# Second attention: three PSUM banks for the turned probabilities and factors, two for the projections

## The chip, the cores and the metric

The kernel runs on one core of one Trainium2 chip. The metric is the device time of one execution in microseconds (us). TensorE (PE in the profile) multiplies matrices and writes its results to PSUM, which has eight banks, each 128 partitions by 512 float32 values. VectorE (DVE) and ScalarE (ACT) read the banks; GpSimd (POOL) works in SBUF alone here; SyncE (SP) issues the loads of weights.

## The reference

Two blocks run one after the other on 512 tokens of width 1024. The first (gated linear attention, stick-breaking attention, an MLP) is not touched. The second, cut to what matters:

```python
def nsa_mixer(h, w_in, w_out, k_pos, k_w1, k_w2, v_pos, v_w1, v_w2, table):
    q, kv, g, z = split_cols(h @ w_in, [NSA_WIDTH, 6 * NSA_KV_WIDTH, 3 * H, 3 * NSA_WIDTH])
    k_c, v_c, k_s, v_s, k_w, v_w = [...]
    gates = jax.nn.sigmoid(g).reshape(B, S, 3, H, 1)
    zs = jax.nn.silu(z).reshape(B, S, 3, H, dh)
    kc = compress_kv(k_c, k_pos, k_w1, k_w2)
    vc = compress_kv(v_c, v_pos, v_w1, v_w2)
    o_cmp, p_cmp = nsa_compressed(q, kc, vc, table)
    o_slc = nsa_selected(q, k_s, v_s, select_blocks(p_cmp, S), table)
    o_win = nsa_window(q, k_w, v_w, table)
    o = jnp.stack([o_cmp, o_slc, o_win], axis=2)
    y = jnp.sum(gates * o * zs, axis=2).reshape(B, S, NSA_WIDTH)
    return y @ w_out
```

There are 16 heads in 4 groups. `z` holds one gate projection for each of the three branches: 24 products of 128 columns by 512 tokens, for 8 pairs of heads `p` and 3 branches `br`.

## The kernel before

The second attention is the function `nsa`. Everything on TensorE there stands in one order, written out by the program: the pieces of attention itself, and between them a **filler** (the class `Filler`), which deals out the steps of the remaining projections so that TensorE always has something to do. TensorE works through its instructions strictly in that order. The orders of VectorE and ScalarE are made by a scheduler when the program is built.

One **unit** of attention (class `Unit`) is a head and a branch. `scores` multiplies queries and keys into a bank of the ring `sc` (lines 1217, 1218); VectorE takes the minimum (L1220) and ScalarE the exponential into `P` (L1223). Two steps later `flip` turns `P` by multiplications with the identity into a bank of the ring `tp` (L1237); ScalarE copies it out as the high part of `ptall` (L1240) and VectorE subtracts that for the low part (L299, names `ptall<-b,ptall`). Later `mix` multiplies it with the values into bank 6 (L1253).

The **filler's** steps are projections of eight k-tiles with three multiplications each (L339, L340, L341, by `gen_t`). `project(p, br)` makes one gate projection: its bank comes from `pj`, and when it is full, ScalarE takes the tanh of it (L995) and VectorE multiplies (L296, names `z<-z,b`). Only then is the bank free. Keys and queries are projected in the same way (their readings are L853 and L875 on ScalarE, L296 `q<-b,q` on VectorE), and `cmp_hidden` (L942 to L944) makes the hidden layer of the compression in a bank of `pj`, woven into a projection by `both`.

Small pieces are hung into a projection by `weave`: after the third of its eight steps (`SH` and `FH` are 2) comes `cmp_scores` (L1050) or `cmp_flip` (L1080). Their bank comes from `mx`, which is the same ring as `pj`. `combine(p)` says which projection of a pair has one. `gate_flip` (L1135), `gate_scale` (L1145) and `finish` (L1092) multiply gate factors and take their banks from `tp`.

A ring deals out its banks in turn, whoever asks:

```python
            bank, sc, tp, av = ring(0, 1, 7), ring(2, 3), ring(4, 5), ring(6)
...
            mx = bank
...
                elif p == 2:
                    order = ((1, {FH: lambda: flip(0)}), (2, score(1, 0)), (0, score(1, 1)))
```

The first multiplication into a bank waits until the last reader of what the bank held has ended, and everything behind it on TensorE waits as well.

Of the kernel before, what the change touches and what calls it, by code (L numbers as in the profile page):

```python
# [245 lines left out]
def emit(gen):  # L246
    for _ in gen:
        pass
# [3 lines left out]
def tile_blocks(ctx, tc, x, xt, wts, prm, cst, table, post_g, w2k, w2v, out):  # L252
# [5 lines left out]
    W = Weights(nc, glob, wts)  # L258
    banks = ctx.enter_context(tc.tile_pool(name="banks", bufs=1, space=PSUM))

    def ring(*ids):
        turn = [0]

        def take():
            i = ids[turn[0] % len(ids)]
            turn[0] += 1
            return banks.tile([128, T], F32, name=f"b{i}", tag=f"b{i}", bufs=1)
        return take
# [20 lines left out]
    def ts(out_, in_, s1, s2=None, op0=OP.mult, op1=None, eng=None):  # L289
        if s2 is None:  # L290
            (eng or v).tensor_scalar(out_, in_, s1, None, op0)
        else:
            (eng or v).tensor_scalar(out_, in_, s1, s2, op0, op1)  # L293

    def stt(out_, a, sc, b, op0, op1):
        v.scalar_tensor_tensor(out_, a, sc, b, op0, op1)  # L296

    def tt(out_, a, b, op=OP.mult, eng=None):
        (eng or v).tensor_tensor(out_, a, b, op)  # L299

    def hi_lo(hi, lo, src, hi_in=None, scale=None):
        if scale is None:
            s.copy(hi, src)
            tt(lo, src, hi.bitcast(F32), OP.subtract)
        else:
            s.activation(hi, src, AF.Identity, scale=scale)
            stt(lo, src, scale, hi.bitcast(F32), OP.mult, OP.subtract)
# [18 lines left out]
    def act_tiles(kt):  # L326
        h = glob.tile([128, T], F32R, name=f"ah{kt}", tag="ah", bufs=8)
        l = glob.tile([128, T], F32R, name=f"al{kt}", tag="al", bufs=8)
        return h, l
# [22 lines left out]
    def gen_n(psum, acts, evac, tail=1, w=512):  # L352
        n = len(acts) // 2
        ps = [psum() for _ in range(4)]
        held = []
        for k2 in range(n):
            wh, wl = W.next()
            if k2 < n - tail:
                order = [(k2, wh, wl, k, tb) for k in range(2) for tb in range(4)]
            else:  # L360
                held.append((k2, wh, wl))
                if k2 < n - 1:
                    continue
                order = [(*w, k, tb) for tb in range(4) for w in held for k in range(2)]
            for kk, wh, wl, k, tb in order:
                ah, al = acts[2 * kk + k]
                tsl = slice(128 * tb, 128 * tb + 128)
                a = wh[:, w * k:w * k + w]
                b = wl[:, w * k:w * k + w]
                o = ps[tb][:, 0:w]  # L370
                end = kk == n - 1 and k == 1
                pe.matmul(o, ah[:, tsl], a, start=(kk == 0 and k == 0), stop=False)  # L372
                pe.matmul(o, ah[:, tsl], b, start=False, stop=False)  # L373
                W.last = pe.matmul(o, al[:, tsl], a, start=False, stop=end)  # L374
                if end:
                    evac(tb, ps[tb])
                yield 650.0
# [403 lines left out]
    def nsa(x2, ssq2):  # L781
# [3 lines left out]
        kst, qst = {}, {}  # L785
        with ExitStack() as pts:
            pt = pts.enter_context(tc.tile_pool(name="pt", bufs=1))
            bank, sc, tp, av = ring(0, 1, 7), ring(2, 3), ring(4, 5), ring(6)

            opened, when, used = [0], [0], [0]  # L790

            def pj():
                opened[0] += 1
                when[0] = fill.ticks
                return bank()

            mx = bank

            acts = [act_tiles(kt) for kt in range(KT)]
# [50 lines left out]
            def keys_evac(gq):  # L850
                def evac(ps):
                    ks = tmp("ks")
                    s.copy(ks, ps)  # L853
                    for br in range(2):
                        kh = pn.tile([128, T], F32R, name="kh", tag="kh", bufs=4)
                        kl = pn.tile([128, T], F32R, name="kl", tag="kl", bufs=4)
                        src = ks[64 * br:64 * br + 64, :]
                        same = slice(64 * br, 64 * br + 64)
                        for d_ in range(2):
                            s.copy(kh[64 * d_:64 * d_ + 64, :], src)  # L860
                        for d_ in range(2):
                            tt(kl[64 * d_:64 * d_ + 64, :], src, kh[same, :].bitcast(F32), OP.subtract)
                        kst[gq, br] = (kh, kl)
                return evac
# [4 lines left out]
            def queries_evac(m):  # L869
                def evac(ps):  # L870
                    for e in range(2):
                        q = pn.tile([128, T], F32R, name="q", tag="qy", bufs=QB)
                        a = slice(64 * e, 64 * e + 64)
                        b = slice(64 - 64 * e, 128 - 64 * e)
                        s.activation(q[a, :], ps[a, :], AF.Copy, scale=-0.125)  # L875
                        stt(q[b, :], ps[a, :], -0.125, q[a, :].bitcast(F32), OP.mult, OP.subtract)
                        qst[2 * m + e] = q
                return evac
# [4 lines left out]
            def values(br):  # L883
                def evac(tb, ps):
                    src = ps[:, 0:256].rearrange("p (g d) -> p g d", g=4)
                    hi = vst[:, tb, 4 * br:4 * br + 4, 0:64]
                    gs = gn[:, tb, 24 * br:24 * br + 24]
                    s.activation(gs, ps[:, 256:280], AF.Tanh, scale=0.5)
                    ts(gs, gs, 0.25, 0.25, OP.mult, OP.add)
                    s.copy(hi, src)  # L890
                    tt(vst[:, tb, 4 * br:4 * br + 4, 64:128], src, hi.bitcast(F32), OP.subtract)
                emit(gen_n((ring(3, 4, 5, 6), ring(2, 0, 1, 7))[br], acts, evac, w=280))
                if br == 0:
                    ts(gn[:, 0, 0:16], gn[:, 0, 0:16], valid)

# [55 lines left out]
                yield 1300.0  # L951

            def cmp_middle(th):
                pst = mx()
                for k in range(2):
                    pe.transpose(pst[:, 128 * k:128 * k + 128], th[:, 128 * k:128 * k + 128], ident)
                hT = pt.tile([128, 256], F32, name="hT", tag="z", bufs=ZB)
                ts(hT, pst[:, 0:256], 0.5)
                return hT
# [1 line left out]
            pct = {}  # L961

            def cmp_output(i, hT, w2):
                o = mx()
                for k in range(2):
                    if i == 0:
                        pe.matmul(o[:, 0:128], w2[:, k, :], hT[:, 128 * k:128 * k + 128],
                                  start=(k == 0), stop=(k == 1))
                    else:
                        pe.matmul(o[:, 0:64], hT[:, 128 * k:128 * k + 128], w2[:, k, :],  # L970
                                  start=(k == 0), stop=(k == 1))
                if i == 0:
                    hi_lo(kc[:, :, 0, :], kc[:, :, 1, :], o[:, 0:128].rearrange("p (g c) -> p g c", g=4))
                else:
                    vc = glob.tile([128, 128], F32, name="vc", tag="dg", bufs=2)[:, 0:64]
                    v.tensor_copy(vc, o[:, 0:64])
                    tc.keep_in_program_order(g.memset(vcb, 0.0))
                    pct["v"] = vc
# [30 lines left out]
            def early():  # L1009
                st = {}  # L1010

                def middle():
                    st["hT"] = cmp_middle(st["th"])

                def output(i):
                    cmp_output(i, st["hT"], st[i])
                Fs, st[0] = yield from compress(0)
                yield from both(cmp_hidden(Fs, st), project(0, 0))
                Fs, st[1] = yield from compress(1, ({2: middle}, {2: lambda: output(0)}))
                started[0] = True  # L1020
                yield from both(cmp_hidden(Fs, st), queries(4))
                yield from weave(keys(2), {2: middle, 5: lambda: output(1)})
                spread_values(0)
                spread_values(1)
# [237 lines left out]
            def attention(fill):  # L1262
# [70 lines left out]
                while pend_flip or pend_mix:  # L1333
# [4 lines left out]
                    pend_mix += new  # L1338

            first = [(pj(), W.next(1), keys_evac(0)), (pj(), W.next(1), queries_evac(0)),  # L1340
                     (mx(), W.next(1), queries_evac(1))]
            enter(0)
            for kt in range(KT):
                if kt == ENTER:
# [11 lines left out]
            for br in range(2):  # L1356
                values(br)
# [38 lines left out]
    with tc.manual_schedule(engines={mybir.EngineType.PE, mybir.EngineType.Pool}):  # L1396
        nsa(xb, sums2)
# [55 lines left out]
```

## Time and profile before

| what | us |
|---|---|
| median of 3 runs | 1370.8 (1369.51 to 1370.91) |
| the profiled execution | 1372.04 |
| its span, first to last instruction | 1370.3 |
| TensorE busy in the span | 1324.2 (97%) |
| VectorE, ScalarE, GpSimd busy | 728.0, 656.0, 273.7 |
| second attention with its filler, 938 to 1320 us: TensorE busy | 359.34 of 382.00 |

A row of the timeline says when an instruction started (us from the start of the span), how long it took, its engine, line, operation, and what it writes from what; in square brackets stands how long its engine had been idle, and what ended that. Names of PSUM buffers are cut to `b`.

### The profile page before, as it was taken

The numbers are of one execution on the slowest core, as the hardware profiler recorded it, in microseconds if no ns is written. First come the engines' busy times: TensorE is split into PE (matmuls) and PEld (weight loads), VectorE is DVE, ScalarE is ACT, GpSimd is POOL, SyncE is SP. The second block draws the span as 40 slices with busy tenths as digits, with TensorE's granted clock in tenths as the row PEclk, the third lists the DMA queues.
The fourth block names the chain that finished last, engine by engine and source line by source line (L and its number), as shares of the span: only waits on it lengthen the run. The fifth ranks groups of instructions, "written<-read, shape, count | busy, mean of one in ns | idle before, by whom it ended". The sixth has DMA issues, their size and how long they took to land.

```text
span 1370.3 us, 17904 instructions
## 1 busy us (share of the span) xinstructions
PE 1324.2 (97%) x6670; PEld 1090.5 (80%) x6670; DVE 728.0 (53%) x1386; ACT 656.0 (48%) x1281; POOL 273.7 (20%) x243
## 2 busy tenths in 40 slices
PE   9999999999999999999999999999888999999998
PEld 7977887777786888888888888888667788888776
DVE  4689435656567535342233322545785766665623
ACT  6588624544434326351135512355556556665532
POOL 0023101110101000000000000145536344335342
PEclk9999999999999999999999999999999999999999
DMA  7411221213131424863333324323313122211132
GB/s 236 139 46 49 76 93 55 85 62 93 51 103 47 155 61 133 125 183 94 96 102 93 95 94 129 118 64 119 94 55 111 52 63 62 70 62 63 47 108 77
DMA packets 40695, 125.31 MB, mean 91 GB/s; under 512 B 4528, under 2 KB 9184, under 8 KB 40352
## 3 DMA queue, kind: packets, MB, share of 16 engines
q1 hardware_dynamic: 39696, 119.98, 27.7%
q0 software_dynamic: 912, 4.19, 2.3%
q8 instruction: 52, 0.85, 0.3%
q14 instruction: 35, 0.29, 0.1%
HBM read 115.77 MB, written 8.39 MB: 91 GB/s over the span
## 4 chain that ended last, share of the span: by engine, by line
PE 66%; issue 15%; DVE 10%; ACT 5%; POOL 2%; DMA 1%; SPq 0%; POOLq 0%; DVEq 0%; ACTq 0%
PE b L374 9%; PE b L372 9%; PE b L373 9%; PE b L339 9%; PE b L340 9%; PE b L341 9%; PE b L1253 2%; PE b L1237 2%; DVE b L1220 1%; DVE ptall L299 1%; ACT P L1223 1%; PE b L1217 1%; PE b L828 1%; PE b L1218 1%; DMA xk<-in_xt_dram 1%
## 5 line engine op out<-in xcount | busy, mean ns | idle before, releaser
L171 ACT CAST wh<-wr 128x1024 fp32r<-128x1024 f32 (+3 forms) x204 | 207.8, 1019 | 403.1 <-PE b L374 225.6
L339 PE MATMUL b<-ah,wh 128*128 128x512 f32 x808 | 331.9, 411 | 2.8 <-ACT ks L853 2.4
L173 DVE TENSOR_TENSOR wl<-wr,wh 128x1024 fp32r<-128x1024 f32 (+2 forms) x142 | 169.5, 1195 | 296.9 <-ACT wh L171 296.4
L341 PE MATMUL b<-ah,wl 128*128 128x512 f32 x808 | 317.4, 393 | 0.0
L340 PE MATMUL b<-al,wh 128*128 128x512 f32 x808 | 317.0, 392 | 0.0
L173 POOL TENSOR_TENSOR wl<-wr,wh 128x1024 fp32r<-128x1024 f32 (+1 forms) x62 | 141.8, 2292 | 192.3 <-ACT wh L171 168.3
L341 PEld LDWEIGHTS b<-ah,wl 128*128 128x128 f32 x808 | 152.2, 188 | 32.4
L339 PEld LDWEIGHTS b<-ah,wh 128*128 128x128 f32 x808 | 152.6, 189 | 30.6 <-ACT ks L853 2.6
L340 PEld LDWEIGHTS b<-al,wh 128*128 128x128 f32 x808 | 152.8, 189 | 25.4 <-issue 1.9
L372 PE MATMUL b<-wh,ah 128*128 128x512 f32 (+3 forms) x352 | 125.5, 358 | 1.6 <-ACT wh L171 1.1
L373 PE MATMUL b<-wl,ah 128*128 128x512 f32 (+3 forms) x352 | 125.4, 356 | 0.1
L374 PE MATMUL b<-wh,al 128*128 128x512 f32 (+3 forms) x352 | 125.3, 356 | 0.1
L1223 ACT ACTIVATE P<-b,nm 128x128 f32<-128x128 f32 (+3 forms) x128 | 67.7, 529 | 80.3 <-DVE nm L1220 77.0
L374 PE MATMUL b<-wh,hl 128*128 128x512 f32 x256 | 101.2, 396 | 0.0
L373 PE MATMUL b<-wl,hh 128*128 128x512 f32 x256 | 101.2, 395 | 0.0
L372 PE MATMUL b<-wh,hh 128*128 128x512 f32 x256 | 101.2, 395 | 0.0
L299 DVE TENSOR_TENSOR ptall<-b,ptall 128x128 fp32r<-128x128 f32 (+3 forms) x128 | 62.5, 489 | 62.3 <-ACT ptall L1240 61.4
L1220 DVE CUSTOM_DVE_ANT_0 b<-b,bt 128x128 f32<-128x128 f32 (+3 forms) x128 | 63.1, 494 | 24.4 <-PE b L1218 24.2
L372 PEld LDWEIGHTS b<-wh,ah 128*128 128x128 f32 x352 | 66.2, 188 | 9.9 <-ACT wh L171 1.3
L374 PEld LDWEIGHTS b<-wh,al 128*128 128x128 f32 x352 | 66.4, 189 | 8.4 <-DVE al L296 0.5
L373 PEld LDWEIGHTS b<-wl,ah 128*128 128x128 f32 x352 | 66.4, 189 | 8.4 <-DVE wl L173 0.5
L299 POOL TENSOR_TENSOR rsr<-rsm,mhalf 128x2 f32<-128x2 f32 (+1 forms) x3 | 2.4, 806 | 336.1 <-DVE rsm L293 336.1
(301 smaller groups left out, 2163.7 us busy)
## 6 DMA issues: line engine op xcount, KB each, us to landing
wr<-in_wts_dram SPq DMA_DIRECT2D x188, 512.0 KB, 3.6
bt_d<-tr POOLq DMA_DIRECT2D x4, 768.0 KB, 21.9
wr<-in_wts_dram SPq DMA_DIRECT2D x8, 280.0 KB, 2.6
xk<-in_xt_dram SPq DMA_DIRECT2D x8, 256.0 KB, 3.8
xn<-in_x_dram SPq DMA_DIRECT2D x4, 512.0 KB, 4.7
xbig<-in_x_dram SPq DMA_DIRECT2D x1, 2048.0 KB, 9.4
x_d<-xbig SPq DMA_DIRECT2D x8, 256.0 KB, 3.1
bt<-bt_d SPq DMA_DIRECT2D x8, 256.0 KB, 3.2
```

The lines of the kernel that those rows point to most:

```text
L171: nc.scalar.copy(hi, raw)
L173: eng.tensor_tensor(lo, raw, hi.bitcast(F32), OP.subtract)
L299: (eng or v).tensor_tensor(out_, a, b, op)
L339: pe.matmul(o, a, ah, start=(kt == 0), stop=False)
L340: pe.matmul(o, a, al, start=False, stop=False)
L341: pe.matmul(o, b, ah, start=False, stop=(kt == KT - 1))
L372: pe.matmul(o, ah[:, tsl], a, start=(kk == 0 and k == 0), stop=False)
L373: pe.matmul(o, ah[:, tsl], b, start=False, stop=False)
L374: W.last = pe.matmul(o, al[:, tsl], a, start=False, stop=end)
L1220: v.tensor_tensor_reduce(S[:, 0:n], S[:, 0:n], self.bt[:, h % 2, 512 - n:512], 1.0, -NEG, OP.add, OP.min, nm)
L1223: latest[0] = s.activation(P[:, 0:n], S[:, 0:n], AF.Exp, bias=nm, scale=-1.0, accum_out=self.dn[:, tb, br, h % 2:h % 2 + 1])
L1237: pe.transpose(pst[:, 128 * sb:128 * sb + 128], P[:, 128 * sb:128 * sb + 128], ident)
```

## The change

The rings of the second attention are dealt differently: bank 7 goes from `bank` (projections, compressed scores, turned compressed probabilities) to `tp` (turned probabilities, turned gate factors, products of the factors). Two small users of `mx`, `cmp_middle` and `cmp_output`, now ask `tp`. The third of the three projections that start the block takes bank 6 instead of bank 7, and so the two sets of rings for `values` exchange 6 and 7.

```diff
-            bank, sc, tp, av = ring(0, 1, 7), ring(2, 3), ring(4, 5), ring(6)
+            bank, sc, tp, av = ring(0, 1), ring(2, 3), ring(4, 5, 7), ring(6)
...
-                emit(gen_n((ring(3, 4, 5, 6), ring(2, 0, 1, 7))[br], acts, evac, w=280))
+                emit(gen_n((ring(3, 4, 5, 7), ring(2, 0, 1, 6))[br], acts, evac, w=280))
...
             def cmp_middle(th):
-                pst = mx()
+                pst = tp()
...
             def cmp_output(i, hT, w2):
-                o = mx()
+                o = tp()
...
             first = [(pj(), W.next(1), keys_evac(0)), (pj(), W.next(1), queries_evac(0)),
-                     (mx(), W.next(1), queries_evac(1))]
+                     (av(), W.next(1), queries_evac(1))]
```

No instruction is added or removed, and TensorE's order stays as it was. What moves is the bank that each writes, and with it what each waits for. In the rows below `b7_8900` is bank 7, buffer 8900, and the brackets name the engine whose count is waited for.

TensorE, where the first gate projection of pair 1 (`b0_8785`) ends and the second begins, before:

```order
L339 MATMUL b0_8785<-ah6_6867,wh_8570 128x512
L340 MATMUL b0_8785<-al6_6868,wh_8570 128x512
L341 MATMUL b0_8785<-ah6_6867,wl_8571 128x512
L1237 MATMUL b4_8871<-ident_65,P_8737 128x128 [waits DVE_49]
L339 MATMUL b0_8785<-ah7_6869,wh_8570 128x512
L340 MATMUL b0_8785<-al7_6870,wh_8570 128x512
L341 MATMUL b0_8785<-ah7_6869,wl_8571 128x512
L1217 MATMUL b2_8886<-kh_7274,q_7192 128x128 [waits Activation_49]
L1218 MATMUL b2_8886<-kl_7275,q_7192 128x128
L339 MATMUL b7_8900<-ah0_6855,wh_8623 128x512
```

And the same place of the changed kernel:

```order
L339 MATMUL b0_8785<-ah6_6867,wh_8570 128x512
L340 MATMUL b0_8785<-al6_6868,wh_8570 128x512
L341 MATMUL b0_8785<-ah6_6867,wl_8571 128x512
L1237 MATMUL b4_8871<-ident_65,P_8737 128x128
L339 MATMUL b0_8785<-ah7_6869,wh_8570 128x512
L340 MATMUL b0_8785<-al7_6870,wh_8570 128x512
L341 MATMUL b0_8785<-ah7_6869,wl_8571 128x512
L1217 MATMUL b2_8886<-kh_7274,q_7192 128x128 [waits Activation_49]
L1218 MATMUL b2_8886<-kl_7275,q_7192 128x128
L339 MATMUL b0_8900<-ah0_6855,wh_8623 128x512 [waits DVE_49]
```

The turning of probabilities (L1237) lost its wait for VectorE; the second projection now begins in bank 0, which the first has just filled, and waits for VectorE.

TensorE where `cmp_hidden` of the keys opens its bank, before:

```order
L339 MATMUL b0_7866<-ah1_6857,wh_7579 128x512
L340 MATMUL b0_7866<-al1_6858,wh_7579 128x512
L341 MATMUL b0_7866<-ah1_6857,wl_7580 128x512
L1237 MATMUL b5_7873<-ident_65,P_7744 128x128 [waits DVE_49]
L1237 MATMUL b5_7873<-ident_65,P_7744 128x128 x3
L942 MATMUL b1_7880<-wh_7633,Fh_7730 128x256
```

The same rows of the changed kernel:

```order
L339 MATMUL b0_7866<-ah1_6857,wh_7579 128x512
L340 MATMUL b0_7866<-al1_6858,wh_7579 128x512
L341 MATMUL b0_7866<-ah1_6857,wl_7580 128x512
L1237 MATMUL b7_7873<-ident_65,P_7744 128x128 [waits DVE_49]
L1237 MATMUL b7_7873<-ident_65,P_7744 128x128 x3
L942 MATMUL b1_7880<-wh_7633,Fh_7730 128x256 [waits DVE_49]
```

The hidden layer stays in bank 1, but with two banks in the ring that bank is the one of the projection just before it, and the first multiplication waits for VectorE.

VectorE's order moves by a place or two at eight places; the one at the end of the second projection of pair 1 (`z<-z,b_8900`) as a piece of the difference:

```order
 L299 TENSOR_TENSOR Pc<-Pc,rgc 128x512
-L1220 ISA b_9007,nm<-b_9007,bt 128x128
-L1220 ISA nm 128x1
 L296 SCALAR_TENSOR_TENSOR z<-z,b_8900 128x512
 L299 TENSOR_TENSOR ptall<-b_8992,ptall 128x128
+L1220 ISA b_9007,nm<-b_9007,bt 128x128
+L1220 ISA nm 128x1
```

The reading that frees a projection's bank moved ahead of the minimum over one tile of scores.

## Rows read from the trace of the kernel before

**Rows 1.** The page, busy time by engine.

```profile
PE 1324.2 (97%) x6670; PEld 1090.5 (80%) x6670; DVE 728.0 (53%) x1386; ACT 656.0 (48%) x1281; POOL 273.7 (20%) x243
```

**Rows 2.** Busy times of the second attention: PE, PEld, DVE, ACT, POOL, clock, DMA, GB/s.

```profile
938.00:1320.00 382.00, 359.34 (x2045) 301.34 (x2044) 257.51 (x638) 226.20 (x554) 161.85 (x98) 0.99 0.22 68
```

**Rows 3.** Waits of TensorE from 938 to 1320 us: total, times, longest.

```profile
PE b L1237 <- DVE ptall L299: 7.6, 12, 1.6
PE b L1135 <- DVE ptall L299: 5.3, 2, 3.5
PE b L339 <- ACT ks L853: 2.4, 1, 2.4
PE b L1253 <- DVE t L299: 2.3, 2, 1.5
...
PE b L1092 <- DVE z L299: 0.9, 1, 0.9
PE b L1145 <- DVE ptall L299: 0.8, 1, 0.8
PE b L1145 <- DVE z L299: 0.4, 1, 0.4
```

**Rows 4.** Timeline where the first projection of pair 1 ends.

```profile
1067.46 0.39 PE L341 MATMUL b<-ah,wl 128*128 128x512 f32 x1
...
1067.87 0.45 PE L339 MATMUL b<-ah,wh 128*128 128x512 f32 x1
...
1067.97 1.06 ACT L171 CAST wh<-wr 128x1024 fp32r<-128x1024 f32 x1
...
1068.92 0.61 ACT L995 ACTIVATE z<-b 128x512 f32<-128x512 f32 x1
...
1069.56 0.69 DVE L296 SCALAR_TENSOR_TENSOR z<-z,b 128x512 f32<-128x512 f32 x1 [0.89 <-ACT z L995]
```

**Rows 5.** Timeline at three other such places: the first, one more, the last.

```profile
989.47 0.47 PE L339 MATMUL b<-ah,wh 128*128 128x512 f32 x1
...
991.37 0.68 DVE L296 SCALAR_TENSOR_TENSOR z<-z,b 128x512 f32<-128x512 f32 x1
...
1080.02 0.69 DVE L296 SCALAR_TENSOR_TENSOR z<-z,b 128x512 f32<-128x512 f32 x1 [0.31 <-ACT z L995]
...
1292.54 0.48 PE L339 MATMUL b<-ah,wh 128*128 128x512 f32 x1
...
1294.36 0.69 DVE L296 SCALAR_TENSOR_TENSOR z<-z,b 128x512 f32<-128x512 f32 x1
```

**Rows 6.** Timeline where the two hidden layers of the compression open their banks.

```profile
969.89 0.66 PE L1237 MATMUL b<-ident,P 128*128 128x128 f32 x4 [1.57 <-DVE ptall L299]
970.30 0.37 PE L942 MATMUL b<-wh,Fh 128*128 128x256 f32 x1
...
975.55 0.68 DVE L296 SCALAR_TENSOR_TENSOR z<-z,b 128x512 f32<-128x512 f32 x1
...
1022.73 0.33 PE L1237 MATMUL b<-ident,P 128*128 128x128 f32 x1 [0.60 <-DVE ptall L299]
...
1022.81 0.36 PE L942 MATMUL b<-wh,Fh 128*128 128x256 f32 x1
...
1026.93 0.69 DVE L296 SCALAR_TENSOR_TENSOR z<-z,b 128x512 f32<-128x512 f32 x1
```

**Rows 7.** Timeline at the third `cmp_flip`, and the late reading of the last queries.

```profile
1222.23 0.60 PE L1080 MATMUL b<-ident,Pc 128*128 128x128 f32 x4
...
1224.74 0.69 DVE L296 SCALAR_TENSOR_TENSOR q<-b,q 64x512 fp32r<-64x512 f32 x1 [0.26 <-ACT q L875]
```

**Rows 8.** Three stretches of 3.4 us, columns as in rows 2.

```profile
1026.05:1029.46 3.41, 1.03 (x7) 0.79 (x8) 3.19 (x10) 1.32 (x3) 1.77 (x2) 1.00 0.00 0
1029.46:1032.88 3.42, 3.42 (x14) 2.92 (x13) 0.42 (x1) 2.29 (x7) 3.42 (x2) 0.55 0.20 31
...
1060.18:1063.60 3.42, 3.42 (x23) 2.96 (x22) 3.31 (x8) 2.60 (x8) 0.00 (x0) 1.00 0.45 153
```

## The prediction, made before the changed kernel was run

> **What bounds the kernel now.** I began with the busy times of the page: TensorE works 97% of the span [rows 1], so any new wait on it is paid nearly in full, and only waits that it has now can be won back. The change touches the second attention, so I cut that stretch out: 359.3 of 382.0 us are busy [rows 2], which leaves 22.7 us to win at the very most. Then the waits of TensorE in that stretch [rows 3]. The reader is to see that nearly all of them end with VectorE, and most at L1237 and L1135, which write banks of `tp`. Last, the timeline at each place where TensorE opens a bank of the projections: there it stands beside the reader that frees what the new ring would hand it. None of these places has a large wait now, since with three banks the one handed out was left long before.
>
> **What is taken away.** With banks 4, 5 and 7 a turned tile comes back to its bank one take later. The waits at L1237 (7.6), L1135 (5.3), L1092 (0.9) and L1145 (0.8 and 0.4) are for readers of `tp` banks, and the single one at L339 for the keys (2.4) is for bank 0, which the new dealing hands out elsewhere; together 17.4 us [rows 3]. The 2.3 us at L1253 are for bank 6, which no edit relieves. Not all of 17.4 is a gain: the waits of 1.57 and 0.60 us at L1237 stand right ahead of L942 [rows 6], which will itself wait for a fixed moment on VectorE (below), so coming there earlier gives nothing. I take 17.4 - 2.2 = **15.2 us won**.
>
> **What is added.** With two banks in turn, a projection comes back to its own predecessor's bank whenever exactly one other tile was taken in between. `combine` shows how often: eight `cmp_scores` and four `cmp_flip` sit inside a projection, so twelve projections are followed by one in the same bank; two more follow a projection into which `cmp_hidden` was woven. That is 14 places. At the worked one the old projection's last multiplication starts at 1067.46 and the next projection's first at 1067.87 [rows 4]. The bank's last reader is VectorE's L296, which ends at 1069.56 + 0.69 = 1070.25. A multiplication starts some 0.05 us after such an end, an estimate from the order of the starts in the timeline. So the new wait is 1070.30 - 1067.87 = 2.43 us. It is made of the tanh (0.61) and the product (0.69), and of what ScalarE has ahead of the tanh: a weight cast of 1.06 us. The first of the 14 gives 991.37 + 0.68 + 0.05 - 989.47 = 2.63, the last 1294.36 + 0.69 + 0.05 - 1292.54 = 2.56 [rows 5]. Read alike, the 14 sum to **31.9 us**, 2.3 on average.
>
> The hidden layers open the bank of the projection that ended before the woven one, and there VectorE is full of the sums `F_`: 975.55 + 0.68 + 0.05 - 970.30 = 5.98 us, and 1026.93 + 0.69 + 0.05 - 1022.81 = 4.86 us [rows 6], together **10.8**. One `cmp_flip` meets the last queries, whose second half is read late: 1224.74 + 0.69 + 0.05 - 1222.23 = **3.25** [rows 7]. The sum of the additions is 31.9 + 10.8 + 3.25 = 46.0 us.
>
> What is queued behind each of these waits is all of TensorE: scores, turnings and mixes stand in the same order. That starves VectorE and ScalarE, but the work they owe at that moment was issued already, and the reader's place in their queues is fixed by the built order, so the wait doesn't shrink by much. The lower bound of one such wait is tanh and product alone behind the last multiplication: 1067.46 + 0.39 + 0.61 + 0.69 + 0.05 - 1067.87 = 1.33 us [rows 4]. I take the measured ends, since the cast that delays the tanh does not depend on TensorE's being ahead.
>
> **The reordering on VectorE** that moves a product ahead of a tile of minima gains nothing where I looked: there the product had waited 0.31 us for the tanh already [rows 5]. **The other edits** (`cmp_middle` and `cmp_output` on `tp`, bank 6 for the third projection, 6 and 7 exchanged in `values`) I cost at nothing: the third bank of `tp` covers the first pair, and if it did not, each would cost about what a turning waits now, 7.6 / 12 = 0.6 us [rows 3]; banks 6 and 7 were last read in the MLP.
>
> **The clock.** After a stretch in which TensorE was busy for only 1.03 of 3.41 us, because it waited for VectorE at L1135, the granted clock falls to 0.55, mostly the lower level of 1.2 GHz, and 14 multiplications are issued where an equal stretch at 2.4 GHz has 23 [rows 8]: 9 x 3.42 / 23 = 1.3 us lost. Ten of the new waits are of 2.4 us or more and lie where the clock does not fall today. I take half of them: 5 x 1.3 = **6.5 us**; the ends are 0 and 13. The Trainium skill (TensorE: Matmul & The Clock Gate, section "Loop structure matters more than you think") says that VectorE's copying of a result out of PSUM between output tiles doesn't break the array's warmth. By that this term would be 0 and the time 1402; the trace disagrees, since the wait ahead of the fall at 1029.46 was for just such a copy.
>
> **The sum.** 46.0 - 15.2 + 6.5 = +37.3 us. The profiled execution took 1372.0 (span 1370.3), so 1409.3; the median lies 1.2 lower than the profiled one, so **1408 us**, 2.7% slower.
>
> **The rivals.**
> *The clock holds* (or falls only where it does now): +30.8, 1401.6. For it: a wait of 2.4 us at L339 stands in rows 3 and is short of the 3.5 us ahead of the one fall that I show. Against: the new waits are many, and close to others. Chance 0.2.
> *The clock falls after every long wait, and waits grow*: 13 instead of 6.5, and the mixes at L1253, whose bank is not relieved, gain some 1 us each after the two hidden layers and the end, an estimate from their longest of 1.5 [rows 3]: +37.3 + 6.5 + 3 = +46.8, 1417.6. The Trainium skill (TensorE: Matmul & The Clock Gate, section "A second HAM failure mode: psum-queue depth-cycling") describes a kernel in which cycling through PSUM banks made the clock swing between its levels. No row here shows such a swing yet. Chance 0.17.
> *Faster.* The one mechanism is that the bank is freed as soon as TensorE holds still, since ScalarE and VectorE then have nothing else to do. It decides from the point where the 17 new waits cost less than the 15.2 won, under 0.9 us each. The lower bound above, 1.33 us, is still over that at the 14 places (18.6), so it needs the tanh to run ahead of the cast and the two long waits to vanish; at 0.5 us each it gives 1370.8 - 15.2 + 8.5 = 1364. Chance 0.03.
> *No change*: new waits and won ones cancel, because the projections' readers come about a microsecond earlier than before: within 2.7 us of 1370.8. Chance 0.03.
> *The forecast*, with some falls of the clock: 1403 to 1414. Chance 0.57.
>
> **The range.** Its lower end takes the rival without falls and shortens 17 waits by 0.2 us: 1401.6 - 3.4, so 1398. Its upper end is the third case with a little more: 1419. The chances: about 0.2% (2.7 us) is what a measurement of this kernel can tell from no change; its three runs lie within 1.4 us. Faster by more 0.03, within it 0.03, slower by more 0.94.
>
> **What would show it.** In the waits of TensorE after the change, a group L339 waiting for VectorE's `z` (L296) with about a dozen cases and 25 to 30 us, one of L942 for the same with two cases and some 11 us, and one at L1080 of about 3 us. The groups L1237 and L1135 for `ptall` should fall from 12.9 us to under 2. The clock should show several more stretches like that at 1029.46 [rows 8], some five behind new waits. The stretch before 938 us should be as it was. I am wrong if the group at L339 is missing or under 12 us; if it is there and the time still is under 1395, the clock and the relief were mis-sized.

## The result, and the profile after

The changed kernel takes 1423.9 us (median of 4 runs, 1420.72 to 1424.55) against 1370.4 before: the ratio is 1.0385, 95% interval 1.0373 to 1.0397. It is 53 us slower; 37 were forecast, and the time lies above the range. The profiled execution took 1424.55 us, its span is 1422.8.

The page's line of busy times and the busy times of the second attention after the change, which answer to [rows 1] and [rows 2]. The stretch runs from 938 us to the same point ahead of the final projection, some 50.5 us before the end of the span.

```profile
PE 1344.7 (95%) x6670; PEld 1108.8 (78%) x6670; DVE 734.7 (52%) x1386; ACT 658.1 (46%) x1281; POOL 273.2 (19%) x243
```

```profile
938.00:1372.00 434.00, 378.35 (x2035) 318.03 (x2034) 262.17 (x637) 228.00 (x552) 158.41 (x96) 0.92 0.19 59
```

The stretch grew from 382.0 to 434.0 us, and that is the whole difference. The reader is to see two parts in it. TensorE stood idle for 434.00 - 378.35 = 55.65 us, before for 382.00 - 359.34 = 22.66: **33.0 us more idle**. And it was busy for 378.35 instead of 359.34 us with the same instructions: **19.0 us more for the same work**. The column of the granted clock says why: 0.92 in place of 0.99.

The waits of TensorE in that stretch, which answer to [rows 3] (total, times, longest):

```profile
PE b L339 <- DVE z L296: 28.0, 13, 2.8
PE b L942 <- DVE z L296: 11.3, 2, 7.5
PE b L1253 <- DVE t L299: 4.4, 3, 2.6
PE b L339 <- DVE q L296: 3.3, 1, 3.3
PE b L1080 <- issue: 3.1, 1, 3.1
PE b L1217 <- ACT P L1223: 2.4, 2, 1.6
PE b L1135 <- DVE gz L299: 1.9, 1, 1.9
PE b L1217 <- DVE vst L299: 0.9, 1, 0.9
PE b L339 <- DVE vst L299: 0.4, 1, 0.4
```

The groups L1237 and L1135 that waited for `ptall` are gone. In their place stands L339 waiting for `z`: 13 projections, 28.0 us, with one more for `q`. With L942 (11.3) and L1080 (3.1, which the view puts down to "issue"; VectorE's second reading of the last queries ends at 1264.79 us and the multiplication starts at 1264.89) the new waits come to 28.0 + 3.3 + 11.3 + 3.1 = 45.7 us; the forecast's sum was 46.0.

The place that was worked out for the forecast [rows 4], after the change:

```profile
1081.19 0.22 PE L1217 MATMUL b<-kh,q 128*128 128x128 f32 x1
1081.24 0.27 PE L1218 MATMUL b<-kl,q 128*128 128x128 f32 x1
1081.76 1.05 ACT L171 CAST wh<-wr 128x1024 fp32r<-128x1024 f32 x1
1082.70 0.61 ACT L995 ACTIVATE z<-b 128x512 f32<-128x512 f32 x1
1083.35 0.69 DVE L296 SCALAR_TENSOR_TENSOR z<-z,b 128x512 f32<-128x512 f32 x1 [0.89 <-ACT z L995]
1084.09 0.50 PE L339 MATMUL b<-ah,wh 128*128 128x512 f32 x1 [2.57 <-DVE z L296]
```

The next projection starts 0.05 us after VectorE's end at 1083.35 + 0.69 = 1084.04, as estimated. TensorE had been idle for 2.57 us; 2.43 was forecast. The cast still stands ahead of the tanh.

What happens next is what the forecast undervalued. Three stretches of the same profile, columns as above (busy time and number of PE, PEld, DVE, ACT, POOL, then the granted clock):

```profile
1084.47:1087.88 3.41, 3.41 (x13) 2.82 (x12) 0.42 (x1) 0.37 (x1) 0.84 (x1) 0.50 0.46 120
1088.00:1091.41 3.41, 3.41 (x25) 3.06 (x25) 2.24 (x6) 1.55 (x4) 0.00 (x0) 1.00 0.05 19
```

```profile
1026.44:1040.09 13.65, 9.18 (x33) 7.91 (x34) 9.93 (x25) 6.81 (x15) 6.47 (x5) 0.50 0.06 16
```

Right behind the wait the clock is at 1.2 GHz, and 13 multiplications fit where the stretch after it holds 25. Around the second hidden layer the clock falls during one wait (2.65 us for `t` at L1253) and stays at 1.2 GHz for 13.65 us on end, through the next (3.83 us for `z` at L942). The mean granted clock of the whole span is 0.975, before 0.995. Time at half speed is twice what is missing to 1: 2 x 0.025 x 1422.8 = 71 us, before 2 x 0.005 x 1370.3 = 14 us. Read place by place, the second attention has 13 places at 1.2 GHz, 68 us together; before there were 3, 10 us together.

### The profile page after: what moved, and what is told of

Read it like the earlier page. It is cut to its first block, busy times and chain, and to the rows that moved or that the text cites. A ratio compares the mean times of both kernels' runs of the same rounds, so it can differ in the third digit from the quotient of the medians.

```text
span 1422.8 us, 17918 instructions
## 1 busy us (share of the span) xinstructions
PE 1344.7 (95%) x6670; PEld 1108.8 (78%) x6670; DVE 734.7 (52%) x1386; ACT 658.1 (46%) x1281; POOL 273.2 (19%) x243
## 4 chain that ended last, share of the span: by engine, by line
PE 67%; issue 15%; DVE 10%; ACT 5%; POOL 2%; DMA 1%; SPq 0%; DVEq 0%; POOLq 0%; ACTq 0%
PE b L339 9%; PE b L340 9%; PE b L341 9%; PE b L372 9%; PE b L374 9%; PE b L373 9%; PE b L1253 2%; PE b L1237 2%; DVE b L1220 1%; PE b L1217 1%; PE b L1218 1%; PE b L828 1%; ACT wh L171 1%; ACT P L1223 1%; DMA xk<-in_xt_dram 1%
## 5 line engine op out<-in xcount | busy, mean ns | idle before, releaser
L339 PE MATMUL b<-ah,wh 128*128 128x512 f32 x808 | 337.2, 417 | 32.1 <-DVE z L296 28.0
L341 PE MATMUL b<-ah,wl 128*128 128x512 f32 x808 | 321.6, 398 | 0.0
L340 PE MATMUL b<-al,wh 128*128 128x512 f32 x808 | 321.0, 397 | 0.0
L339 PEld LDWEIGHTS b<-ah,wh 128*128 128x128 f32 x808 | 154.8, 192 | 63.9 <-DVE z L296 31.4
L1240 ACT CAST ptall<-b 128x128 fp32r<-128x128 f32 (+3 forms) x128 | 53.8, 422 | 29.4 <-PE b L1237 28.4
```

Source lines behind the costliest of these rows:

```text
L339: pe.matmul(o, a, ah, start=(kt == 0), stop=False)
L340: pe.matmul(o, a, al, start=False, stop=False)
L341: pe.matmul(o, b, ah, start=False, stop=(kt == KT - 1))
```

## The experiments

Each time is a median beside runs of the kernel before on the same chip, which gave 1370.4 to 1370.8. "Idle" and "busy" are TensorE's from 938 us to some 50.5 us before the end of the span, read from one row of busy times each as above.

| kernel | us | ratio, 95% interval | stretch | busy | idle |
|---|---|---|---|---|---|
| before | 1370.4 | | 382.0 | 359.3 | 22.7 |
| changed | 1423.9 | 1.0373 to 1.0397 | 434.0 | 378.4 | 55.7 |
| changed, again | 1420.0 | 1.0333 to 1.0389 | 425.8 | 368.5 | 57.3 |
| bank 7 idle | 1416.2 | 1.0325 to 1.0357 | 424.7 | 368.9 | 55.8 |
| bank 7 idle, again | 1416.0 | 1.0310 to 1.0351 | 426.3 | 370.4 | 55.9 |
| bank 7 idle, filled | 1405.7 | 1.0246 to 1.0277 | 413.1 | 388.8 | 24.3 |
| changed, filled | 1407.4 | 1.0250 to 1.0281 | 417.8 | 393.1 | 24.7 |
| scores on the ring of three | 1391.5 | 1.0134 to 1.0164 | 401.4 | 364.1 | 37.3 |
| all small pieces on it | 1377.1 | 1.0040 to 1.0068 | 389.4 | 361.5 | 27.9 |
| and hidden layer late | 1366.6 | 0.9959 to 0.9980 | 376.5 | 357.3 | 19.2 |
| the same, bank 7 idle | 1387.9 | 1.0113 to 1.0144 | 397.6 | 366.7 | 31.0 |
| before, hidden layer late | 1378.4 | 1.0044 to 1.0069 | 388.2 | 361.8 | 26.4 |

My theory after the result: the waits are as forecast, and the time beyond them is the clock. The rival: the extra time is in something that the third bank or the waits do to the other engines.

**The taking alone.** Projections lose bank 7, and nobody gets it.

```diff
-            bank, sc, tp, av = ring(0, 1), ring(2, 3), ring(4, 5, 7), ring(6)
+            bank, sc, tp, av = ring(0, 1), ring(2, 3), ring(4, 5), ring(6)
```

> The changed kernel, but the third bank is not given to the turned probabilities: projections have banks 0 and 1, the turned tiles 4 and 5, bank 7 lies idle. If relief and new waits simply add (as I forecast), the 15 us won go as well: about 1424 + 15 = 1439. If the relief is mostly swallowed by the new waits, because a tensor engine that stands still at a projection anyway gives VectorE time to catch up, only some 3 us are lost: 1425 to 1430, with the waits of L1237 and L1135 for ptall not returning in full.

Measured: 1416.2 us, so both expectations missed: without the third bank the kernel is not slower but faster. Its waits, the first rows of the view:

```profile
PE b L339 <- DVE z L296: 28.1, 13, 2.7
PE b L942 <- DVE z L296: 10.2, 2, 5.7
PE b L1237 <- DVE ptall L299: 4.6, 6, 1.6
PE b L1080 <- issue: 3.1, 1, 3.1
PE b L1253 <- DVE t L299: 2.7, 2, 1.5
PE b L1135 <- DVE ptall L299: 1.8, 1, 1.8
```

L1237 and L1135 are back with 6.4 us, not with the 12.9 of [rows 3], and all the idle time is 55.8 us, the same as with the third bank (55.7). What the third bank takes away here comes back at L942 (11.3 for 10.2), at L339 for `q` (3.3 for 1.0), at L1253 (4.4 for 2.7) and at L1135 for `gz` (1.9). So beside the new waits the relief is worth nothing. The 8 us between the two kernels are in the busy time, 378.4 against 368.9 in these two profiles; a second profile of each (below) has 368.5 and 370.4, so this difference is not a fixed property of the kernels.

**Filling the waits.** On the kernel with bank 7 idle, TensorE multiplies into that bank ahead of the places that wait; nobody reads the result.

```diff
             def pj(spin=0):
...
+                if held[0] == t.name[:2] and opened[0] > 6:
+                    spin = SPIN
+                for _ in range(spin):
+                    pe.matmul(idle, acts[0][0][:, 0:128], acts[0][0], start=True, stop=True)
...
-                hp = pj()
+                hp = pj(20)
```

> The kernel with bank 7 idle, and ahead of the twelve projections that come back to the bank just filled TensorE does 9 multiplications into the idle bank (9 x 0.23 = 2.1 us), ahead of the two hidden layers 20 (4.6 us). Nobody reads them. The work is nearly as long as the wait that it stands in. If the clock is what made the change cost 53 us instead of 37 (17 more falls), this kernel is 12 to 20 us faster than the one with the bank idle, with fewer than 10 stretches at 1.2 GHz in the second attention. If the extra time is in the waits themselves or in engines that are starved behind them, it is as slow or up to 5 us slower.

Measured: 1405.7 us, 10.5 less than without the filling, a little under the 12 to 20 expected. The worked place in its timeline (the lines of the file are a few higher, L803 is the filling):

```profile
1072.39 2.27 PE L803 MATMUL b<-ah 128*128 128x512 f32 x9
...
1074.37 0.69 DVE L297 SCALAR_TENSOR_TENSOR z<-z,b 128x512 f32<-128x512 f32 x1 [0.89 <-ACT z L1005]
...
1075.12 0.50 PE L340 MATMUL b<-ah,wh 128*128 128x512 f32 x1 [0.46 <-DVE z L297]
```

```profile
938.00:1351.10 413.10, 388.83 (x2192) 324.52 (x2191) 258.55 (x637) 228.47 (x554) 160.17 (x96) 1.00 0.21 63
```

The wait is as long as before, but 2.27 us of it are filled, and the granted clock of the stretch is 1.00 (it was 0.96). A kernel became faster by 148 more multiplications. They take some 34 us (0.23 each), so the 388.8 us of busy time hold about 355 us of the kernel's own work, 14 less than without the filling (368.9). The time in which TensorE can't go on with its own work did not shrink: 24.3 idle and 34 filled make 58, where 55.8 were idle. So the gain is in the pace of the same multiplications, and that is the clock.

**Filling with the third bank.** The same on the changed kernel, into the bank that the ring of three deals out next.

```diff
+                idle = tp() if spin else None
                 for _ in range(spin):
                     pe.matmul(idle, acts[0][0][:, 0:128], acts[0][0], start=True, stop=True)
```

> The changed kernel with its third bank, and the same multiplications for nobody ahead of the twelve returns (9) and the two hidden layers (20), written into the bank that the ring of three deals out next. If the third bank costs time through the clock alone (20 stretches at 1.2 GHz against 10 with the bank idle), it must be no slower here than the 1405.7 of the kernel with idle bank and the same filling: 1398 to 1407, with at most 3 slow stretches. If the third bank hurts in another way, such as work of VectorE drawn ahead, it stays some 8 us over that: 1411 to 1416.

Measured: 1407.4 us, just over what the clock theory allowed (1398 to 1407, and no slower than 1405.7) and well under 1411 to 1416. The clock is not held up quite as well as with the idle bank: 0.98 in the second attention, with two places at 1.2 GHz, where the other had 1.00 and none. With the filling the third bank is 1.7 us behind. The changed kernel became 16.5 us faster by gaining work, 12.6 against its repeat below, which ran on the same chip.

**The two once more, on one chip.** Nothing is edited.

> The changed kernel once more, beside the kernel with bank 7 idle on one chip. If the third bank by itself makes things worse through more slow stretches, 1420 to 1425 here and 4 to 9 us over the idle one. If the difference was one of chips, they come out within 2 us.

> The kernel with bank 7 idle once more: 1414 to 1420 if it is the kernel, within 2 us of the changed kernel's if it was the chip.

Measured: 1420.0 us (1416.07 to 1425.55) and 1416.0 (1414.29 to 1418.91). The difference is 4 us, the lower edge of the first expectation, and the single executions tell what it is. Span and mean granted clock of each:

```
changed       1422.8 0.975   1422.0 0.977   1419.0 0.980   1422.4 0.977
changed again 1414.3 0.983   1418.7 0.980   1423.8 0.975   1417.8 0.980
bank 7 idle   1413.2 0.987   1414.3 0.984   1418.7 0.980   1414.6 0.984
idle again    1414.8 0.984   1412.6 0.984   1417.2 0.983   1413.8 0.983
idle, filled  1401.6 0.999   1405.0 0.995   1403.4 0.996   1404.6 0.997
```

At 0.980 the changed kernel takes 1417.8 to 1419.0 and the one with the idle bank 1418.7; at 0.983 both take 1413.8 to 1417.2. The same program spreads over 9.5 us with its clock. So the third bank adds no time of its own at a given clock. Over eight executions each, four of them side by side on one chip, the changed kernel has a mean clock of 0.978 and a mean span of 1420.1 us, the kernel with the idle bank 0.984 and 1414.9 us. So the third bank seems to draw the clock down a little; through what is not shown.

How much the execution decides shows in the second profile of the changed kernel. The reader is to see the same place in both, the one after the worked place: the wait in brackets, then the 6.83 us from 0.47 us ahead of its end (the last column but two is the clock). First the profile of the result:

```profile
1098.59 0.80 PE L339 MATMUL b<-ah,wh 128*128 128x512 f32 x1 [2.67 <-DVE z L296]
1098.12:1104.95 6.83, 6.36 (x17) 5.10 (x18) 2.03 (x6) 0.83 (x3) 2.65 (x2) 0.50 0.23 79
```

And the second profile, with its whole stretch:

```profile
1097.57 0.50 PE L339 MATMUL b<-ah,wh 128*128 128x512 f32 x1 [2.67 <-DVE z L296]
1097.10:1103.93 6.83, 6.36 (x36) 5.47 (x37) 3.19 (x9) 2.27 (x7) 2.68 (x2) 1.00 0.24 79
938.00:1363.80 425.80, 368.53 (x2044) 310.52 (x2043) 263.07 (x637) 228.50 (x554) 159.76 (x96) 0.95 0.20 61
```

After the same wait of 2.67 us the clock is down in one execution, with 17 multiplications, and up in the other, with 36. The second profile has 8 places at 1.2 GHz, 44 us together, for 13 places and 68 us in the first, and the lower clock costs it 368.53 - 359.34 = 9.2 us, not 19.0. Its idle time is no shorter (57.3 us). So a wait of given length does not settle whether the clock falls.

**A third of the returns.** Only the scores move to the ring of three, so that four of the twelve projections with a small piece inside still have their successor in the same bank.

```diff
-                S = mx()
+                S = tp()
```

> The changed kernel, but only the eight compressed scores take their banks from the ring of three; the four turned compressed probabilities stay with the projections. Of the twelve returns four are left. If each return costs its wait of 2.2 us and about 0.8 slow stretches of 1.2 us, between the 1423.9 of all twelve and the 1377.1 of none this lies at 1388 to 1396, with 9 to 14 slow stretches. If the cost is not in the single returns, it is not near a third of the way.

Measured: 1391.5 us, in the middle of the range. L339 waits for `z` five times, 9.6 us: the four returns and the one behind a hidden layer. The cost is in the single returns.

**None of the returns.** All small pieces move there.

```diff
-            mx = bank
+            mx = tp
```

> The changed kernel, but the compressed scores and the turned compressed probabilities also take their banks from the ring of three, so that projections alternate between 0 and 1 with nothing in between. If the twelve returns to the bank just filled are the cause, the waits of L339 for z fall from 28 us to under 4 and the one at L1080 goes; the two hidden layers keep their 11 us. Time 1368 to 1376. If two banks are simply too few for projections, whatever is dealt in between, the waits at L339 stay above 15 us and the time above 1395.

Measured: 1377.1 us, a microsecond over. Its waits:

```profile
PE b L942 <- DVE z L296: 11.4, 2, 7.5
PE b L1253 <- DVE t L299: 4.4, 3, 2.6
PE b L339 <- DVE q L296: 3.4, 1, 3.4
PE b L1217 <- ACT P L1223: 2.4, 2, 1.6
PE b L339 <- DVE z L296: 2.3, 1, 2.3
```

L339 for `z` fell from 28.0 to 2.3 and L1080 is gone. Two banks are enough for the projections; what was too much was a short piece dealt out between two of them.

**The hidden layer late.** On top of that, `both` starts `cmp_hidden` after the sixth of the eight steps; its pieces then follow after every step instead of every second one.

```diff
             def both(a, b):
                 for k, ns in enumerate(b):
                     yield ns
-                    if k % 2 == 1:
+                    if k >= 5:
```

> As the kernel with the small pieces on the ring of three, and the hidden layer of the compression starts after the sixth of the eight steps of the projection that it is woven into (before: after the second), so that the bank it takes has been read by then. If the waits at L942 are for the reading alone, they shrink from 11 us to under 4 and the time is 1361 to 1367, under the kernel before. If what follows (VectorE's sums of the compression) is only late elsewhere, it is 1368 to 1374.

Measured: 1366.6 us, ratio 0.9970 (0.9959 to 0.9980) to the kernel before: this version beats both. L942 is out of its waits altogether:

```profile
PE b L1253 <- DVE t L299: 8.0, 4, 3.3
PE b L1135 <- DVE gz L299: 4.2, 1, 4.2
PE b L1217 <- ACT P L1223: 3.0, 4, 1.6
PE b L1237 <- DVE ptall L299: 2.0, 1, 2.0
```

Idle time is 19.2 us, less than before's 22.7. Part of the gain came back at L1253 (8.0 for 4.4 us) and L1135 (4.2 for 1.9), which wait for other work of VectorE.

**What the third bank is worth without the new waits.** The last kernel with bank 7 idle, so that turned tiles and small pieces share two banks.

```diff
-            bank, sc, tp, av = ring(0, 1), ring(2, 3), ring(4, 5, 7), ring(6)
+            bank, sc, tp, av = ring(0, 1), ring(2, 3), ring(4, 5), ring(6)
```

> The kernel with the small pieces on the ring of the turned tiles and the late hidden layer, but that ring has banks 4 and 5 alone; bank 7 lies idle. There the new waits are gone, so the third bank shows its own worth. If it frees TensorE of waits that nothing else takes over, this is 8 to 15 us slower than the 1366.6 with it, with L1237 and L1135 waiting for ptall and z again. If its relief turns up as other waits for VectorE anyway, within 3 us of 1366.6.

Measured: 1387.9 us, 21 more, beyond the 8 to 15 expected.

```profile
PE b L1237 <- DVE ptall L299: 9.6, 12, 2.7
PE b L1135 <- DVE ptall L299: 5.3, 2, 3.5
PE b L1253 <- DVE t L299: 3.0, 2, 1.5
PE b L1135 <- DVE gz L299: 2.9, 1, 2.9
```

The waits for `ptall` that the third bank lifts stand there again, 14.9 us (2.0 with it). Of the 21 us, 31.0 - 19.2 = 11.8 are idle time and 366.7 - 357.3 = 9.4 are slower multiplication. The bank that is worth nothing beside the new waits is worth this much without them, but here with the small pieces in the same ring; how much of the 21 us is theirs is not separated.

**The late hidden layer on the kernel before.** The edit to `both` alone.

> The kernel before with the hidden layer started after the sixth step and nothing else. If the late start alone made the gain of 4 us, 1365 to 1368. If it needs the dealing with three banks for turned tiles, no gain: 1369 to 1375.

Measured: 1378.4 us, slower than either expectation. So the 4 us gained are not the late start's alone. Its idle time is 3.7 us over before's, its busy time 2.5. In its waits L1135 for `gz` is new (2.9 us) and L1217 for `P` is longer (3.4 for 1.6); what delays these was not followed up.

## Why the prediction was wrong

- **The mechanism, and who waits for whom: right.** The same-bank returns were 13 for `z` and one for `q`, as counted: 31.3 us where 31.9 stood. The two hidden layers took 11.3 for 10.8, the turned piece 3.1 for 3.25. That the sums meet so closely is partly luck: the hidden layers waited 7.46 and 3.83 us where 5.98 and 4.86 stood, and the return behind the queries that the second one is woven into waited 3.35 us, where the same reading of the trace before gives 1.22. The three kernels that take the returns and the hidden layers away one after the other (37.3, 27.9 and 19.2 us idle) show that these are the causes.
- **The relief: right as a sum, wrong in its reason.** Old waits fell from 22.5 to 10.0 us by the view of waits, 12.5 where I put 15.2. But 9 of them fall without the third bank too: with bank 7 idle, 13.3 are left. It fits that a TensorE that already stands at a projection gives VectorE the time to catch up. I let 2.2 us be swallowed by a wait behind; in truth all that the third bank lifts was. The idle time came to +33.0 us, forecast 30.8.
- **The clock: this is the step that failed.** I wrote "I take half of them: 5 x 1.3 = 6.5 us; the ends are 0 and 13". Measured in the profile of the result are 19.0 us, over the upper end too, and the 12.5 us beyond the 6.5 are most of the 15 by which the stretch missed the sum (+52.0 for +37.3). In this profile the clock fell 11 times outside the two hidden layers, not five, and three of these falls lasted 6.83 us; around the hidden layers it was low for 20.5 us (6.8 before). The price was about right: four profiles of the changed kernel and of the one with bank 7 idle give 0.27 to 0.40 us lost per us at the lower clock, and 1.3 over 3.42 is 0.38. The number was wrong for three reasons. I counted at most one fall for each of ten waits, yet the clock stays low through the next wait when one is near, for 13.65 us in the longest case. I left out the two hidden layers, because the clock falls there already before the change; the fall there is now longer. And I reasoned from one fall, behind a wait of 3.5 us, while the trace before had another behind a wait of 1.84 us, shorter than any of the ten:

```profile
1314.53 0.66 PE L1135 MATMUL b<-ident,gz 128*128 128x128 f32 x4 [1.84 <-DVE ptall L299]
1316.50:1319.91 3.41, 3.41 (x13) 2.93 (x13) 1.97 (x3) 0.59 (x1) 2.66 (x3) 0.50 0.45 96
```

- **How far the miss was luck.** The second profile of the changed kernel has 6 falls outside the hidden layers and 9.2 us lost, inside my 0 to 13, and took 1416.07 us, inside the range. It was the fastest of eight executions; the other seven took 1419.5 to 1425.6. A single number for this term was not to be had: it differs by 10 us from execution to execution.
- **The copy out of PSUM.** The forecast cited the Trainium skill (TensorE: Matmul & The Clock Gate, section "Loop structure matters more than you think"), by which a copy out of PSUM between output tiles doesn't break the array's warmth. Its sketch lets the next tile's multiplications follow at once. Where the next tile opens in the bank that is being read they can't, and there the trace shows falls, as behind the wait that ends at 1084.09, though not behind every such wait. Where TensorE has something else to multiply meanwhile the trace agrees, as the filled kernels show (clock 0.993 to 0.999). The 1402 that the forecast drew from the Trainium skill was 22 us short.
- **The rivals.** "The clock holds" is refuted by the profile and is what the filled kernels bring about. "The clock falls after every long wait" was the nearest, with 1418 and a chance of 0.17, and still below: its clock term was 13 for 19.0 us, its growth at L1253 3 for 2.1. "Faster" and "no change" failed as the bank was not freed sooner; at the worked place the cast of weights stayed ahead of the tanh.
- **The other edits** cost next to nothing: attention starts at 939.50 us (L1217; 940.37 before), and the one new wait at its start is 0.4 us at L339 for `vst`.

## What to carry to other kernels

A ring that two kinds of user share decides not by its size but by who asks in between: with two banks, one short piece between two long ones sends the second long one into the bank that is just being read, and here moving the short pieces to another ring won back 47 us (43 against the repeat) without a bank more. Count an in-order engine's new waits and old ones as one chain, since relief among longer waits was worth nothing here. And where many waits of 2 to 3 us are added to TensorE, price the lower clock by the time that it lasts (here 0.27 to 0.40 us per us), including the waits that it runs through, not by one fall each. Give that term a wide range, since the same kernel lost 9.2 us in one profile and 19.0 in another.

## What the runs showed of the hardware

Multiplications whose result nobody reads made the kernel 10.5 us (bank 7 idle) and 12.6 to 16.5 us (changed) faster, because they held the granted clock up through most waits: its mean over the span is 0.995 to 0.999 where it was 0.980 to 0.987, and 0.993 to 0.994 where it was 0.975 to 0.983. Executions of one program on one chip differ in their mean clock, 0.975 to 0.983 for the changed kernel, and their spans follow it, 1423.8 to 1414.3 us; behind the same wait of 2.67 us the clock fell in one profile and not in another. The kernel before, with few waits and a clock of 0.993 to 0.997, spreads over 3 to 4 us in 7 to 11 runs on a chip.
